# Attention scores of a two-layer decoder trunk from three or four products a head instead of four, with the weight splits held back earlier

## The chip, the core and the metric

The kernel runs on one core of one Trainium2 chip. The metric is the device time of one execution in microseconds (us); lower is better. Before the change the median of three runs was 938.75 us, the lowest 937.65 and the highest 941.82.

## What is computed

A trunk of two layers for one sequence of 256 tokens of width 1024, in float32. Cut to its order:

```python
for layer in range(2):
    h = h + 0.5 * swiglu(rms_norm(h, ffn1_norm[layer]), ...)     # width 2816
    hn = rms_norm(h, mix_norm[layer])
    h = h + (ab_mixer(hn, ...) if layer == 0 else c_mixer(hn, ...))
    h = h + 0.5 * swiglu(rms_norm(h, ffn2_norm[layer]), ...)
return rms_norm(h, final_norm)
```

The first mixer has 8 causal attention heads of width 64 (three dilated windows, folded into one additive mask of log counts) beside a gated branch (gelu, norm, causal mixing of positions). The second mixer has 16 causal heads of width 64. In both, a head needs scores q k^T, a masked softmax, and the weighted sum of v. With 256 queries in two blocks of 128, block 0 attends to 128 keys and block 1 to 256.

## The kernel before, in words

**Numbers in two parts.** TensorE multiplies in its fast float32 form (fp32r), which drops bits. So each operand is held as a rounded high part and a low part (the rest), and `mm3` (L265 to L268) adds three products, high with high, low with high, high with low. ScalarE (ACT) makes the high part by a copy, VectorE (DVE) the low part by a subtraction.

**The weight stream.** `Stream` (L115) loads the weights in chunks of 1 MB in the order in which they are used, into three raw buffers, by DMA from the SP queue. `split_parts` (L147) turns a chunk into its two parts (`whi` by ACT on L172, `wlo` by DVE on L173), in one of four buffers each. A chunk can be split when the chunk four places ahead of it has been used (`pump`, L186). `hold` (L196) stops splitting; `release` (L200) splits one chunk, or lets all that is due go again, and places these instructions behind some given ones.

**The order of the work.** A mixer is written as a sequence of projections on TensorE (PE), with attention steps put between them by hand: `Slots` (L747) counts steps, each of some 2.7 us of projection matmuls (half that in the last four), and at each step calls what was put down for it: `scores` of a head, `turn` of a head (three transposes of its probabilities and their split into `pth` and `ptl`), `weighted` of a pair of heads (their products with v, split into `mixh` and `mixl`). The tile framework then orders each engine's instructions; every engine works its list in order. In the first mixer, steps 0 to 3 are `first_tiles`, 4 to 11 two `token_block`s, 12 to 19 four weight chunks of two steps each, and 20 to 27 `project` (L388), the output projection. In the second, steps 4 to 7 and 16 to 19 are token blocks, 24 to 31 `project`. `project` ends with `nxt.pair` (L308), which adds the result to the residual (L312, DVE) and makes the next stage's `xTh` (L302, ACT) and `xTl` (L305, DVE); the next feed-forward stage starts on these.

**The scores.** A pair of heads shares a tile of 128 partitions, 64 for each head. `put_q` (L665) makes the head's `q` tile: the high part on its own 64 partitions (L672, ACT) and a copy of it on the other 64 (L674, GpSimd, called POOL); and a tile `ql` with the low part on its own 64 partitions and zeros on the others (L673, DVE). `put_k` (L677) makes `k`: the high part on the head's own partitions (L683, ACT), the low part on the others (L685, POOL or DVE). So one product with `q` gives high by high plus high by low, and one with `ql` gives low by high. `scores` (L690) does both for each of two query blocks, four matmuls with 256 columns (L700, L701). Then for each block DVE adds the mask and takes the row's minimum of the negated scores (L704), ACT takes the exponential and its sum (L707), DVE the reciprocal (L710), and POOL, or DVE for the last heads, scales the probabilities (L714).

**Before the change** the first mixer puts scores of heads 0 to 3 at steps 6 to 9 and of 4 to 7 at 20, 20, 21, 21, turns at 10, 10, 12, 12, 22, 22, 23, 23, `hold` at 19, and releases at 21 (one chunk, behind the scores of head 7), 22 (one, behind turn 5) and 25 (all, behind the last `weighted`). The second mixer has no hold of its own.

Of the kernel before, what the change touches and what calls it, by code (L numbers as in the profile page):

```python
# [35 lines left out]
LINE, SHIFT = 64, 16  # L36
# [188 lines left out]
def trunk(ctx: ExitStack, tc: tile.TileContext, a, out):  # L225
    nc = tc.nc
# [418 lines left out]
    def make_attention(mp, mask_cols, nheads, v, mix, rows=False):  # L645

        qs, ks, probs, pts = {}, {}, {}, {}
        pairs, flying = (4, 5) if rows else (2, 4)
        seconds = [mp.tile([128, 2 * S + LINE], F32R, name=f"ql{i}") for i in range(pairs)]
        for t in seconds:  # L650
            for j in range(2):
                o = slice(64 - j * 64, 128 - j * 64)
                nc.gpsimd.memset(t[o, SHIFT + j * S : SHIFT + (j + 1) * S].bitcast(F32), 0.0)  # L653
        mask = mp.tile([128, 384], F32, name="mask")
        nc.scalar.dma_start(mask, a["consts"][:, mask_cols])

        def scaled(bk):
            t = mp.tile([128, S], F32, name="qk", bufs=3)
            nc.vector.tensor_mul(t, bk[:, :S], norm["row"])
            return t  # L660

        def sides(j):
            return slice(j * 64, j * 64 + 64), slice(64 - j * 64, 128 - j * 64)

        def put_q(p, bk):  # L665

            t = bk[:, :S] if rows else scaled(bk)
            qq = mp.tile([128, 2 * S + LINE], F32R, name="q", bufs=pairs)
            for j in range(2):
                q, ql = (u[:, SHIFT + j * S : SHIFT + (j + 1) * S] for u in (qq, seconds[p % pairs]))  # L670
                r, o = sides(j)
                nc.scalar.activation(q[r, :], t[r, :], AF.Copy)  # L672
                nc.vector.tensor_sub(ql[r, :], t[r, :], q[r, :].bitcast(F32))  # L673
                nc.gpsimd.tensor_copy(q[o, :], q[r, :].bitcast(F32))  # L674
                qs[2 * p + j] = (q, ql)

        def put_k(p, bk):  # L677

            t = scaled(bk)
            for j in range(2):  # L680
                k = mp.tile([128, S], F32R, name=f"k{j}", bufs=pairs)
                r, o = sides(j)
                nc.scalar.activation(k[r, :], t[r, :], AF.Copy)  # L683
                engine = nc.vector if p > 1 and not rows else nc.gpsimd
                engine.tensor_sub(k[o, :], t[r, :], k[r, :].bitcast(F32))  # L685
                ks[2 * p + j] = k
            if p == 1 or p == 3 and not rows:

                nc.scalar.activation(wk.tile([128, 2], F32, name="l")[:, :1], t[:, :1], AF.Exp, scale=0.0)

        def scores(h):
            q, ql = qs.pop(h)
            k = ks.pop(h)
            sc = bank()
            pr = mp.tile([128, 384], F32, name="pr", bufs=flying)
            nm = wk.tile([128, 2], F32, name="nm")
            l = wk.tile([128, 2], F32, name="l")
            for b in range(2):
                bs = slice(b * 128, b * 128 + 128)
                nc.tensor.matmul(sc[:, b * S : (b + 1) * S], q[:, bs], k, start=True, stop=False)  # L700
                nc.tensor.matmul(sc[:, b * S : (b + 1) * S], ql[:, bs], k, start=False, stop=True)  # L701
            for b, (c0, n) in enumerate(((0, 128), (128, 256))):
                cs = slice(c0, c0 + n)
                nc.vector.tensor_tensor_reduce(pr[:, cs], sc[:, b * S : b * S + n], mask[:, cs],  # L704
                                               norm["score"][:, b : b + 1] if rows else -SCALE, 3e38,
                                               op0=ALU.add, op1=ALU.min, accum_out=nm[:, b : b + 1])
                power = nc.scalar.activation(pr[:, cs], pr[:, cs], AF.Exp, bias=nm[:, b : b + 1], scale=-1.0,  # L707
                                             accum_out=l[:, b : b + 1])
            rl = wk.tile([128, 2], F32, name="rl")
            nc.vector.reciprocal(rl, l)  # L710
            for b, (c0, n) in enumerate(((0, 128), (128, 256))):
                cs = slice(c0, c0 + n)
                engine = nc.gpsimd if h < nheads - (4 if rows else 2) else nc.vector
                share = engine.tensor_scalar(pr[:, cs], pr[:, cs], rl[:, b : b + 1], None, op0=ALU.mult)  # L714
            probs[h] = pr
            return power, share

        def turn(h):
            p, j = divmod(h, 2)
            pr = probs.pop(h)  # L720
            tp = bank()
            for i in range(3):
                nc.tensor.transpose(tp[:, i * 128 : (i + 1) * 128], pr[:, i * 128 : (i + 1) * 128], ident)  # L723
# [100 lines left out]
    def ab_mixer(phase):  # L824
        with tc.tile_pool(name="mp", bufs=1) as mp:
# [4 lines left out]
            put_q, put_k, scores, turn, weighted = make_attention(mp, slice(0, 384), 8, v, mix)  # L830
# [38 lines left out]

            slots = Slots()  # L870
            slots.at((15, 16, 16, 17), mixing)
            slots.at((19,), lambda _: st.hold())
            slots.at((6, 7, 8, 9, 20, 20, 21), scores)
            slots.at((21,), lambda _: st.release(tc, scores(7), True))
            slots.at((10, 10, 12, 12, 22), turn)
# [19 lines left out]
    def c_mixer(phase):  # L895
        with tc.tile_pool(name="mp", bufs=1) as mp:
# [93 lines left out]
```

## Time and profile before

| | |
|---|---|
| median of the runs | 938.75 us |
| profiled execution, whole | 937.01 us |
| its span, first to last instruction | 935.3 us |
| PE busy | 927.7 us (99%) |
| DVE busy | 612.1 us (65%) |
| ACT busy | 499.2 us (53%) |
| POOL busy | 83.0 us (9%) |
| first matmul after the first mixer starts at | 277.24 us of the span |
| first matmul after the second mixer starts at | 748.22 us of the span |

The span is the time between the first and the last instruction of one profiled execution; 1.71 us of the whole lie around it. A row of the timeline has the start in us from the span's start, the time in us, engine, line, operation, output and inputs, and the count of instructions that it merges. A matmul's row shows its own time from start to modelled end, which overlaps with the next; what one matmul costs on a busy PE is the distance to the next one's start.

### The profile page before, as it was taken

How to read it: one execution, taken by the hardware profiler on the slowest of the kernel's cores; microseconds unless marked ns; L12 is line 12 of the kernel's file. 1: busy time of each engine (PE TensorE's matmuls, PEld its weight loads, DVE VectorE, ACT ScalarE, POOL GpSimd, SP SyncE). 2: the span in 40 equal slices, each digit the busy share in tenths (PEclk: the TensorE clock that was granted, in tenths of full speed). 3: DMA queues.
4: the chain of work that ended last, by engine and by line, in shares of the span. 5: the costliest groups of instructions: out<-in, count | busy, mean ns of one | idle time of the engine just before them, and what ended most of it. 6: DMA issues, size and time to landing. Idle time of an engine off the chain costs nothing.

```text
span 935.3 us, 18101 instructions
## 1 busy us (share of the span) xinstructions
PE 927.7 (99%) x7655; PEld 907.4 (97%) x7655; DVE 612.1 (65%) x892; ACT 499.2 (53%) x782; POOL 83.0 (9%) x114
## 2 busy tenths in 40 slices
PE   9999999999999999999999999999999999999997
PEld 9999999999999999999999999999999999999886
DVE  7866556676888666555756665567787786656543
ACT  7744444468667454444454544456786665445431
POOL 0000000034210000000000000002574000000000
PEclk9999999999999999999999999999999999999999
DMA  8755554665336555555555555556543377555521
GB/s 320 281 212 181 189 194 162 223 222 180 136 136 226 188 211 188 183 175 206 204 184 200 204 180 170 203 184 220 177 139 136 137 243 269 186 188 210 190 90 46
DMA packets 28305, 176.99 MB, mean 189 GB/s; under 512 B 3264, under 2 KB 4672, under 8 KB 9152
## 3 DMA queue, kind: packets, MB, share of 16 engines
q1 hardware_dynamic: 26928, 173.65, 52.5%
q10 hardware_dynamic: 1296, 2.18, 0.7%
q8 instruction: 60, 0.98, 0.4%
q14 instruction: 21, 0.17, 0.0%
HBM read 173.72 MB, written 2.10 MB: 188 GB/s over the span
## 4 chain that ended last, share of the span: by engine, by line
PE 98%; issue 1%; DMA 0%; ACT 0%; SPq 0%; DVE 0%; POOLq 0%; POOL 0%
PE bank L266 30%; PE bank L267 30%; PE bank L268 30%; PE bank L567 2%; PE bank L571 2%; PE bank L568 2%; PE bank L723 1%; PE bank L700 1%; PE bank L701 1%; DMA x<-in_x 0%; PE bank L343 0%; PE bank L859 0%; PE bank L361 0%; PE bank L455 0%; PE bank L456 0%
## 5 line engine op out<-in xcount | busy, mean ns | idle before, releaser
L172 ACT ACTIVATE whi<-raw 128x1024 fp32r<-128x1024 f32 (+3 forms) x352 | 330.5, 985 | 350.1 <-issue 282.9
L173 DVE TENSOR_TENSOR wlo<-raw,whi 128x1024 fp32r<-128x1024 f32 (+3 forms) x352 | 389.6, 1141 | 126.7 <-ACT whi L172 125.8
L266 PE MATMUL bank<-xTh,whi 128*128 128x256 f32 x1616 | 447.9, 277 | 0.0
L267 PE MATMUL bank<-xTl,whi 128*128 128x256 f32 x1616 | 446.7, 276 | 0.0
L268 PE MATMUL bank<-xTh,wlo 128*128 128x256 f32 x1616 | 446.6, 276 | 0.0
L267 PEld LDWEIGHTS bank<-xTl,whi 128*128 128x128 f32 x1616 | 303.5, 188 | 0.2
L266 PEld LDWEIGHTS bank<-xTh,whi 128*128 128x128 f32 x1616 | 303.5, 188 | 0.0
L268 PEld LDWEIGHTS bank<-xTh,wlo 128*128 128x128 f32 x1616 | 303.5, 188 | 0.0
L267 PE MATMUL bank<-hTl,whi 128*128 128x256 f32 x528 | 145.8, 276 | 0.0
L266 PE MATMUL bank<-hTh,whi 128*128 128x256 f32 x528 | 145.8, 276 | 0.0
L268 PE MATMUL bank<-hTh,wlo 128*128 128x256 f32 x528 | 145.8, 276 | 0.0
L266 PEld LDWEIGHTS bank<-hTh,whi 128*128 128x128 f32 x528 | 99.1, 188 | 0.0
L268 PEld LDWEIGHTS bank<-hTh,wlo 128*128 128x128 f32 x528 | 99.1, 188 | 0.0
L267 PEld LDWEIGHTS bank<-hTl,whi 128*128 128x128 f32 x528 | 99.1, 188 | 0.0
L506 DVE TENSOR_TENSOR hm<-gs,bank 128x512 f32<-128x512 f32 x44 | 30.1, 687 | 77.7 <-PE bank L268 77.3
L503 DVE TENSOR_TENSOR gs<-bank,row 128x512 f32<-128x512 f32 x44 | 30.0, 689 | 47.8 <-PE bank L268 47.8
L266 PE MATMUL bank<-mixh,whi 128*128 128x256 f32 x128 | 35.3, 281 | 0.0
L267 PE MATMUL bank<-mixl,whi 128*128 128x256 f32 x128 | 35.1, 277 | 0.0
L268 PE MATMUL bank<-mixh,wlo 128*128 128x256 f32 x128 | 35.0, 277 | 0.0
L714 POOL TENSOR_SCALAR pr<-pr,rl 128x128 f32<-128x128 f32 (+1 forms) x36 | 30.8, 870 | 25.2 <-DVE rl L710 14.1
L653 POOL MEMSET ql<- 64x256 f32 x12 | 3.7, 307 | 328.7 <-ACT whi L172 170.3
L567 PE MATMUL bank<-whi,hTh 128*128 128x512 f32 x80 | 31.1, 389 | 0.0
(134 smaller groups left out, 877.4 us busy)
## 6 DMA issues: line engine op xcount, KB each, us to landing
raw<-in_weights SPq DMA_DIRECT2D x149, 1024.0 KB, 4.9
raw<-in_weights SPq DMA_DIRECT2D x12, 768.0 KB, 4.4
raw<-in_weights SPq DMA_DIRECT2D x6, 512.0 KB, 6.5
x<-in_x SPq DMA_DIRECT2D x4, 264.0 KB, 4.0
raw<-in_weights SPq DMA_DIRECT2D x4, 256.0 KB, 4.3
away<-xn SPq DMA_DIRECT2D x2, 512.0 KB, 5.5
xr<-away SPq DMA_DIRECT2D x8, 128.0 KB, 5.7
fg<-in_final_norm ACTq DMA_DIRECT2D x1, 512.0 KB, 3.7
```

The costliest lines, as they stand in the source:

```text
L172: nc.scalar.activation(hi, r, AF.Copy)
L173: nc.vector.tensor_sub(lo, r, hi.bitcast(F32))
L266: nc.tensor.matmul(p, sh, mh, start=start, stop=False)
L267: nc.tensor.matmul(p, sh, ml, start=False, stop=False)
L268: nc.tensor.matmul(p, sl, mh, start=False, stop=stop)
L503: nc.vector.tensor_mul(g, both(pg), twice(norm["row"]))
L506: nc.vector.tensor_mul(hm, g, both(pu))
L567: nc.tensor.matmul(banks[t, h], sh, w[0][kw][:, cs], start=k == 0, stop=False)
L568: nc.tensor.matmul(banks[t, h], sh, w[1][kw][:, cs], start=False, stop=False)
L571: nc.tensor.matmul(banks[t, h], sl, w[0][kw][:, cs], start=False, stop=k == FT - 1)
L700: nc.tensor.matmul(sc[:, b * S : (b + 1) * S], q[:, bs], k, start=True, stop=False)
L714: share = engine.tensor_scalar(pr[:, cs], pr[:, cs], rl[:, b : b + 1], None, op0=ALU.mult)
```

## The change

Three edits.

1. **Scores.** In the first mixer for heads 0 to 3, in the second for all 16, `q` holds the high part on the head's own 64 partitions and the low part on the other 64 (one DVE subtraction, no POOL copy, no `ql`). `k` has two halves: in the first the high part on both 64s (ACT, then a POOL copy), in the second the low part on the head's own partitions (a POOL subtraction) and zeros on the others (memset once). One product of `q` with the first half gives high by high plus low by high; one with the second half gives high by low. Query block 0 needs 128 keys only, so one matmul takes the first 128 columns of both halves side by side (256 columns), and a new DVE add (`added`) joins its second 128 columns with the mask before the reduction. Block 1 takes two matmuls. Heads 2 and 10 of the second mixer keep four matmuls and no `added`. Heads 4 to 7 of the first mixer are as before.
2. **First mixer.** `hold` at step 17 instead of 19; the releases stay.
3. **Second mixer.** Scores of heads 7 to 11 one step later; turns of heads 4 and 5 at step 15 instead of 16, of 8 and 9 at 21 instead of 20, of 10 and 11 at 23 instead of 22; `weighted` of pair 2 at 17 instead of 18, of pair 4 at 23 instead of 22, of pair 5 at 25 instead of 24. `hold` at step 24, one chunk released behind the scores of head 15 (step 25), the rest behind turn 15 (step 27).

```diff
         pairs, flying = (4, 5) if rows else (2, 4)
-        seconds = [mp.tile([128, 2 * S + LINE], F32R, name=f"ql{i}") for i in range(pairs)]
-        for t in seconds:
-            for j in range(2):
-                o = slice(64 - j * 64, 128 - j * 64)
+        keys = [[mp.tile([128, 2, S], F32R, name=f"k{i}{j}") for j in range(2)] for i in range(pairs)]
+        seconds = [] if rows else [mp.tile([128, 2 * S + LINE], F32R, name=f"ql{i}") for i in range(2)]
+        for j in range(2):
+            o = slice(64 - j * 64, 128 - j * 64)
+            for pair in keys:
+                nc.gpsimd.memset(pair[j][o, 1].bitcast(F32), 0.0)
+            for t in seconds:
                 nc.gpsimd.memset(t[o, SHIFT + j * S : SHIFT + (j + 1) * S].bitcast(F32), 0.0)
...
+        def early(p):
+
+            return rows or p < 2
...
                 nc.scalar.activation(q[r, :], t[r, :], AF.Copy)
-                nc.vector.tensor_sub(ql[r, :], t[r, :], q[r, :].bitcast(F32))
-                nc.gpsimd.tensor_copy(q[o, :], q[r, :].bitcast(F32))
-                qs[2 * p + j] = (q, ql)
+                if early(p):
+                    nc.vector.tensor_sub(q[o, :], t[r, :], q[r, :].bitcast(F32))
+                    qs[2 * p + j] = q, None
+                else:
+                    ql = seconds[p - 2][:, cs]
+                    nc.vector.tensor_sub(ql[r, :], t[r, :], q[r, :].bitcast(F32))
+                    nc.gpsimd.tensor_copy(q[o, :], q[r, :].bitcast(F32))
+                    qs[2 * p + j] = q, ql
...
-                k = mp.tile([128, S], F32R, name=f"k{j}", bufs=pairs)
+                k = keys[p % pairs][j]
                 r, o = sides(j)
-                nc.scalar.activation(k[r, :], t[r, :], AF.Copy)
-                engine = nc.vector if p > 1 and not rows else nc.gpsimd
-                engine.tensor_sub(k[o, :], t[r, :], k[r, :].bitcast(F32))
+                nc.scalar.activation(k[r, 0], t[r, :], AF.Copy)
+                if early(p):
+                    nc.gpsimd.tensor_copy(k[o, 0], k[r, 0].bitcast(F32))
+                    nc.gpsimd.tensor_sub(k[r, 1], t[r, :], k[r, 0].bitcast(F32))
+                else:
+                    nc.vector.tensor_sub(k[o, 0], t[r, :], k[r, 0].bitcast(F32))
                 ks[2 * p + j] = k
...
             q, ql = qs.pop(h)
+            if rows and h in (2, 10):
+
+                ql = q
...
-            for b in range(2):
-                bs = slice(b * 128, b * 128 + 128)
-                nc.tensor.matmul(sc[:, b * S : (b + 1) * S], q[:, bs], k, start=True, stop=False)
-                nc.tensor.matmul(sc[:, b * S : (b + 1) * S], ql[:, bs], k, start=False, stop=True)
+            if ql is None:
+                nc.tensor.matmul(sc[:, :S], q[:, :128], k[:, :, :128], start=True, stop=True)
+                nc.tensor.matmul(sc[:, S : 2 * S], q[:, 128:], k[:, 0], start=True, stop=False)
+                nc.tensor.matmul(sc[:, S : 2 * S], q[:, 128:], k[:, 1], start=False, stop=True)
+                added = mp.tile([128, 128], F32, name="added", bufs=2)
+                nc.vector.tensor_add(added, sc[:, 128:S], mask[:, :128])
+            elif ql is q:
+                added = mask[:, :128]
+                for i in range(2):
+                    for b in range(2):
+                        nc.tensor.matmul(sc[:, b * S : (b + 1) * S], q[:, b * 128 : (b + 1) * 128], k[:, i],
+                                         start=i == b == 0, stop=i == b == 1)
+            else:
...
-                nc.vector.tensor_tensor_reduce(pr[:, cs], sc[:, b * S : b * S + n], mask[:, cs],
+                nc.vector.tensor_tensor_reduce(pr[:, cs], sc[:, b * S : b * S + n], mask[:, cs] if b else added,
...
-            slots.at((19,), lambda _: st.hold())
+            slots.at((17,), lambda _: st.hold())
...
-            slots.at((5, 6, 7, 8, 12, 13, 14, 15, 16, 17, 18, 19, 24, 24, 25, 25), scores)
-            slots.at((9, 9, 11, 11, 16, 16, 18, 18, 20, 20, 22, 22, 26, 26, 27, 27), turn)
-            slots.at((11, 13, 18, 20, 22, 24, 28, 29), weighted)
+            slots.at((5, 6, 7, 8, 12, 13, 14, 16, 17, 18, 19, 20, 24, 24, 25), scores)
+            slots.at((24,), lambda _: st.hold())
+            slots.at((25,), lambda _: st.release(tc, scores(15), True))
+            slots.at((9, 9, 11, 11, 15, 15, 18, 18, 21, 21, 23, 23, 26, 26, 27), turn)
+            slots.at((27,), lambda _: st.release(tc, turn(15)))
+            slots.at((11, 13, 17, 20, 23, 25, 28, 29), weighted)
```

More of the change, by code (lines that the diff above doesn't have):

```diff
@@ L669, in put_q @@
             for j in range(2):
-                q, ql = (u[:, SHIFT + j * S : SHIFT + (j + 1) * S] for u in (qq, seconds[p % pairs]))
+                cs = slice(SHIFT + j * S, SHIFT + (j + 1) * S)
+                q = qq[:, cs]
                 r, o = sides(j)
                 nc.scalar.activation(q[r, :], t[r, :], AF.Copy)
-                nc.vector.tensor_sub(ql[r, :], t[r, :], q[r, :].bitcast(F32))
-                nc.gpsimd.tensor_copy(q[o, :], q[r, :].bitcast(F32))
-                qs[2 * p + j] = (q, ql)
+                if early(p):
[6 more added lines that the diff above has]
+                    qs[2 * p + j] = q, ql
         def put_k(p, bk):
@@ L697, in scores @@
             l = wk.tile([128, 2], F32, name="l")
-            for b in range(2):
-                bs = slice(b * 128, b * 128 + 128)
-                nc.tensor.matmul(sc[:, b * S : (b + 1) * S], q[:, bs], k, start=True, stop=False)
-                nc.tensor.matmul(sc[:, b * S : (b + 1) * S], ql[:, bs], k, start=False, stop=True)
+            if ql is None:
[11 more added lines that the diff above has]
+            else:
+                added = mask[:, :128]
+                for b in range(2):
+                    bs = slice(b * 128, b * 128 + 128)
+                    nc.tensor.matmul(sc[:, b * S : (b + 1) * S], q[:, bs], k[:, 0], start=True, stop=False)
+                    nc.tensor.matmul(sc[:, b * S : (b + 1) * S], ql[:, bs], k[:, 0], start=False, stop=True)
             for b, (c0, n) in enumerate(((0, 128), (128, 256))):
                 cs = slice(c0, c0 + n)
-                nc.vector.tensor_tensor_reduce(pr[:, cs], sc[:, b * S : b * S + n], mask[:, cs],
+                nc.vector.tensor_tensor_reduce(pr[:, cs], sc[:, b * S : b * S + n], mask[:, cs] if b else added,
                                                norm["score"][:, b : b + 1] if rows else -SCALE, 3e38,
```

## Prediction, made before the changed kernel was run

> **What bounds the kernel.** First the page: busy shares, granted clock, the chain that ended last. Then the windows of the two mixers, the only stages that the change touches.
>
> ```profile
> span 935.3 us, 18101 instructions
> PE 927.7 (99%) x7655; PEld 907.4 (97%) x7655; DVE 612.1 (65%) x892; ACT 499.2 (53%) x782; POOL 83.0 (9%) x114
> PEclk9999999999999999999999999999999999999999
> PE 98%; issue 1%; DMA 0%; ACT 0%; SPq 0%; DVE 0%; POOLq 0%; POOL 0%
> 195.00:290.00 95.00, 94.88 (x722) 90.09 (x722) 75.41 (x162) 66.84 (x146) 26.53 (x33) 1.00 0.45 158
> 645.00:765.00 120.00, 120.00 (x932) 114.86 (x931) 95.83 (x224) 86.09 (x189) 47.03 (x57) 1.00 0.47 165
> ```
>
> TensorE is the bound, at full clock, in both mixers too (94.88 of 95 us and 120 of 120). So an edit is worth what it takes from PE's row of matmuls, less what PE newly waits for. DVE is 79% to 80% busy in these windows (75.41 of 95, 95.83 of 120): work added there can come late. A busy PE can hide a wait shorter than a matmul's own 0.28 us, so I read waits from distances between starts.
>
> **The matmuls that go.** Before, a head has four; after, 4 heads of the first mixer and 14 of the second have three: 18 fewer.
>
> ```profile
> 655.72 0.28 PE L700 MATMUL bank<-k,q 128*128 128x256 f32 x1
> 656.19 0.40 PE L266 MATMUL bank<-whi,xTh 128*128 128x512 f32 x1
> ...
> 679.11 0.28 PE L700 MATMUL bank<-k,q 128*128 128x256 f32 x1
> 679.56 0.28 PE L266 MATMUL bank<-xTh,whi 128*128 128x256 f32 x1
> ...
> L266 PE MATMUL bank<-pth,vth 128*128 128x256 f32 x12 | 3.4, 280 | 0.0
> ```
>
> Four take 0.47 us in a token block (656.19 - 655.72) and 0.45 us elsewhere, 0.118 and 0.113 each. Eight of the 18 lie in token blocks, or after one: 8 x 0.118 + 10 x 0.113 = **-2.07 us**. One of the three reads two strips of 128 columns; the `pth` row above is such a matmul and takes 280 ns like the others, so I add nothing for it. In token blocks the matmuls after a head run a little slow; a new count can move that either way, and I allow 0.5 us on both sides for it. The POOL copy moves from `q` to `k`, 24 before and 24 after (16 of the second mixer and 4 + 4 of the first), and memsets lie where POOL idles (it is 9% busy). The new DVE add counts below, where something waits for it.
>
> **Hold at step 17, what it frees.** Chunk C, the third of the output projection, is no longer split before the scores of heads 4 to 7.
>
> ```profile
> 249.97 1.22 DVE L173 TENSOR_TENSOR wlo<-raw,whi 128x1024 fp32r<-128x1024 f32 x1
> 251.10 0.41 DVE L659 TENSOR_TENSOR qk<-bank,row 128x256 f32<-128x256 f32 x1
> 252.00 0.87 DVE L685 TENSOR_TENSOR k<-qk,k 64x256 fp32r<-64x256 f32 x2 [0.48 <-ACT k L683]
> ...
> 252.17 0.28 PE L268 MATMUL bank<-mixh,wlo 128*128 128x256 f32 x1
> 252.57 0.36 PE L700 MATMUL bank<-k,q 128*128 128x256 f32 x1
> 252.76 0.28 PE L701 MATMUL bank<-k,ql 128*128 128x256 f32 x1
> 252.88 0.28 PE L700 MATMUL bank<-k,q 128*128 128x256 f32 x1
> ```
>
> PE starts head 4 at 252.57, 0.40 after the matmul before it, and then takes 0.19 for one more: 0.36 us over two steps of 0.113. It waits for `k`, which DVE makes at 252.00 behind that half of the split (1.22). Without it `k` comes a microsecond sooner and the wait goes: **-0.36**.
>
> **Hold at step 17, what it defers.** The releases stay, so each lets out the chunk before the one it did: C, D, and at the last two at once, E and F. In the built order of the changed kernel DVE has four `wlo` halves there instead of two, all ahead of the residual adds.
>
> ```profile
> 271.38 2.36 DVE L173 TENSOR_TENSOR wlo<-raw,whi 128x1024 fp32r<-128x1024 f32 x2 [0.66 <-ACT whi L172]
> 273.77 1.29 DVE L312 TENSOR_TENSOR x<-bank,x 128x512 f32<-128x512 f32 x2
> ...
> 277.90 0.87 DVE L305 SCALAR_TENSOR_TENSOR xTl<-x,gT,xTh 128x256 fp32r<-128x256 f32 x2
> ...
> 279.05 0.28 PE L267 MATMUL bank<-xTl,whi 128*128 128x256 f32 x1
> ```
>
> The residual add starts as the second half ends (271.38 + 2.36 = 273.74, add at 273.77), and DVE has no idle time from there to the `xTl` of k = 4 and 5, done at 278.77. PE wants k = 5 at 279.05: 0.28 us to spare. Two more halves cost 2.36 us, so the adds start at 276.1 and that `xTl` is done at 281.1. PE waits 2.36 - 0.28 = **+2.1 us** in the first matmuls of the feed-forward stage. ACT is no later than DVE (its halves take 1.0). C and D come in time: C takes the place where D's `wlo` was, done before its first use. Bounds: 1.0 (one half slips behind the adds) to 2.4.
>
> **Turns of heads 4 and 5 a step sooner, behind longer score chains.**
>
> ```profile
> 687.66 0.17 DVE L710 RECIPROCAL rl<-l 128x2 f32<-128x2 f32 x1
> 688.02 1.50 POOL L714 TENSOR_SCALAR pr<-pr,rl 128x128 f32<-128x128 f32 x2
> 689.69 0.28 PE L700 MATMUL bank<-k,q 128*128 128x256 f32 x1
> 693.37 0.82 PE L723 MATMUL bank<-ident,pr 128*128 128x128 f32 x6
> ...
> L864 DVE TENSOR_TENSOR tmp<-bank,sbias 128x128 f32<-128x128 f32 x8 | 1.9, 280 | 0.3 <-POOL mixl L868 0.3
> L673 DVE TENSOR_TENSOR ql<-bank,q 64x256 fp32r<-64x256 f32 x16 | 6.7, 421 | 0.8 <-ACT q L672 0.4
> ```
>
> Before, head 5's probabilities are scaled at 688.02 to 689.52 and turned at 693.4, 3.9 us later. Now the turn stands at step 15, where head 7's scores stood (689.69), 0.34 sooner for three matmuls gone: 689.35, head 5's from 689.7. And its chain is longer: `added` for heads 4 and 5 (the L864 row is the like: 0.28 each), and head 4's second reduction now behind the second subtraction for `q` (0.42). That is at most 0.98; I take 0.85, since part fits into idle time. Reciprocal at 688.5, scaling done at 690.25; PE has three transposes to do meanwhile and waits **+0.55** (0 to 1.2). A rule weighed here: the Trainium skill, "SBUF — State Buffer", section "Who interferes with whom", says that a DVE instruction with two SBUF inputs and a GpSimd one that reads SBUF exclude each other for the whole instruction. By it a `wlo` in the way would add its 1.2 to 1.5 us; the built order puts none behind that reciprocal, so by the rule the sum is the same, and if it is wrong on that, 1.5 us more.
>
> **Second mixer, last steps.** Turns 14 and 15 stand at step 27 in both. Splits no longer stand between the scores of heads 14 and 15, so their probabilities are ready; now chunk F's split stands behind the turns' `pth` and `ptl`, not before.
>
> ```profile
> 730.81 0.82 PE L723 MATMUL bank<-ident,pr 128*128 128x128 f32 x6
> 734.21 0.90 PE L723 MATMUL bank<-ident,pr 128*128 128x128 f32 x6
> 734.29 2.01 ACT L172 ACTIVATE whi<-raw 128x1024 fp32r<-128x1024 f32 x2 [0.52 <-PE bank L267]
> 735.38 2.36 DVE L173 TENSOR_TENSOR wlo<-raw,whi 128x1024 fp32r<-128x1024 f32 x2 [0.76 <-ACT whi L172]
> 738.59 0.41 DVE L271 TENSOR_TENSOR mixl<-bank,mixh 64x256 fp32r<-64x256 f32 x1
> 739.45 0.43 DVE L271 TENSOR_TENSOR mixl<-bank,mixh 64x256 fp32r<-64x256 f32 x1 [0.45 <-ACT mixh L271]
> 739.81 0.28 PE L266 MATMUL bank<-mixh,whi 128*128 128x256 f32 x1
> 739.93 0.38 PE L267 MATMUL bank<-mixl,whi 128*128 128x256 f32 x1
> 740.15 0.29 PE L268 MATMUL bank<-mixh,wlo 128*128 128x256 f32 x1
> ```
>
> Six transposes take 0.90 at 734.21 and 0.82 at 730.81: the wait of 0.08 goes, **-0.08**. After the turns F's `wlo` begins some 1.3 us later than before (behind two `pth` and two `ptl`), so the last `mixl` of pair 6 comes 0.1 to 0.7 us later against PE. Before, PE already waits for it once: 739.93 to 740.15 is 0.22, 0.11 over. So **+0.3** (0 to 0.7).
>
> **Sum.** -2.07 - 0.36 + 2.1 + 0.55 - 0.08 + 0.3 = +0.44 us. The profiled execution, 937.01 us (span 935.3 and 1.71 around it), becomes 937.45; it lies 1.74 below the median of the runs, 938.75, from which I forecast **939.2 us**: no change, for a measurement of this kernel can tell about 0.5% (4.7 us) from none.
>
> **The rivals.**
>
> *The new waits don't come; only matmuls go.* For it: PE has waited almost nowhere in 920 us, and the terms +2.1 and +0.55 rest on slack that I read to 0.3 us. Against it: the order of the four `wlo` ahead of the adds is fixed, and the adds followed the split by 0.03 us. All that then stays is -2.07 - 0.36 - 0.08 and the 0.11 wait: -2.6, **936.1 us**.
>
> *Slower: POOL comes late for the turn of heads 6 and 7 (step 18).* Head 7's scores move to step 16, its turn stays; behind head 5's scaling POOL has four passes for `k`, head 6's scaling, four more for `k`, and head 7's scaling.
>
> ```profile
> L674 POOL CAST q<-q x24: 392/480/1897, 201.6 to 715.9; 64x256 fp32r<-64x256 f32 x24
> L685 POOL TENSOR_TENSOR k<-qk,k x20: 727/739/1754, 202.9 to 722.8; 64x256 fp32r<-64x256 f32 x20
> L714 POOL TENSOR_SCALAR pr<-pr,rl x36: 602/919/1937, 211.5 to 709.6; 128x128 f32<-128x128 f32 x18, 128x256 f32<-128x256 f32 x18
> ```
>
> At medians that is 4 x 0.480 + 4 x 0.739 + 4 x 0.919 = 8.6 us, from 690.25 to 698.8. PE wants head 7 near 701.2: after 690.6 come three steps of 24 matmuls' time (2.7 each), three heads of 0.35, one `weighted` of 1.0 and head 6's transposes, 0.33. At the longest of each row it is 22.4 us: 11 us late. It decides from 10.9 us. At 15 us PE waits 4.1 more, and the time is **943.3 us**. The rule of the Trainium skill above is what would make these passes long; 1.897 against 0.392 agrees with it, for a `wlo` pass takes 1.2 us. Against it: long passes are rare, or the medians would not lie at the shortest.
>
> *The stacked product doesn't save.* If the matmul on two strips took as long as two, 18 x 0.115 come back: +2.5 in all, **941.3 us**. The `pth` row speaks against it.
>
> **Chances.** Forecast within 1.5 us 0.60; waits don't come 0.22; POOL late 0.11; no saving 0.07. Range for 8 in 10: from the first rival with the 0.5 of the token blocks, 935.6, up to between the third and the second, 942.2. Over 0.5% faster is beyond every case (-2.6 is 0.28%) but for the scatter of the runs: 0.03. Over 0.5% slower needs POOL's rival past its price, or terms at their upper ends with a scatter like that of the slowest run: 0.07. Within: 0.90.
>
> **What the profile after would show.** 7637 matmuls, three to a head. The wait at 252 gone. Four `wlo` in a row before the first L312 of the first mixer, and PE waiting for `xTl` near 278, 2 us in pieces. A wait of about half a microsecond inside the transposes of head 5, none before heads 6 and 7. A pair 6 `mixl` that PE waits for by 0.3. I am wrong if `xTl` is there in time, if L714 of head 7 ends after 701, or if matmuls outside the mixers change their pace.

## The result, and the profile after

The changed kernel takes 940.66 us (median of 20 runs; 940.33 to 941.25) where the kernel before, in 20 runs beside them, takes 937.58. The ratio is 1.003, with a 95% interval of 1.0023 to 1.0037: slower by 0.30%, some 2.8 us. That is inside the 0.5% called no change and inside the forecast's range, but the forecast had +0.4. The forecast of 939.2 us lies only 1.5 us from the measured time, and part of that is luck: it was built on a median of 938.75 us, where the runs beside this one have 937.58. As a change, +0.4 was far too small; several terms of the sum are wrong, and the experiments below are about those. Of several kernels here, the kernel before included, single executions took some 3 to 13 us longer than the rest, and a ratio counts them in, so where ratio and median differ the median is closer to what the traces show.

Page of the changed kernel: span, busy time, chain.

```profile
span 939.2 us, 18072 instructions
PE 927.7 (99%) x7637; PEld 906.1 (96%) x7637; DVE 617.6 (66%) x910; ACT 498.6 (53%) x782; POOL 82.3 (9%) x118
PE 89%; DVE 4%; ACT 3%; issue 1%; POOL 1%; DMA 0%; SPq 0%; POOLq 0%; ACTq 0%; DVEq 0%
```

Its waits of PE from 240 to 770 us (in total, times, longest). The same view of the kernel before lists none there.

```profile
PE bank L756 <- POOL pr L747: 2.0, 3, 0.9
PE bank L756 <- DVE mixl L271: 1.7, 1, 1.7
```

Eighteen matmuls have gone (7637), yet the chain of PE has fallen from 98% to 89%: PE now waits, and others have become part of what ends last. The span grew by 3.9 us. I split that by the distances between starts of matmuls, at the same points of both programs.

**First mixer.** Before head 4 the wait is gone: PE runs straight from the projection into the scores.

```profile
252.17 0.28 PE L268 MATMUL bank<-mixh,wlo 128*128 128x256 f32 x1
252.28 0.28 PE L733 MATMUL bank<-k,q 128*128 128x256 f32 x1
```

Behind the mixer the four halves stand in one row, the adds follow, and PE waits at the first `xTl`. DVE, then PE:

```profile
271.01 4.63 DVE L173 TENSOR_TENSOR wlo<-raw,whi 128x1024 fp32r<-128x1024 f32 x4 [0.66 <-ACT whi L172]
275.67 1.29 DVE L312 TENSOR_TENSOR x<-bank,x 128x512 f32<-128x512 f32 x2
276.94 0.89 DVE L305 SCALAR_TENSOR_TENSOR xTl<-x,gT,xTh 128x256 fp32r<-128x256 f32 x2
```
```profile
276.96 0.38 PE L266 MATMUL bank<-xTh,whi 128*128 128x256 f32 x1
277.48 0.39 PE L267 MATMUL bank<-xTl,whi 128*128 128x256 f32 x1
...
278.23 0.44 PE L266 MATMUL bank<-xTh,whi 128*128 128x256 f32 x2
...
288.96 0.50 PE L343 MATMUL bank<-ones,acc 128*128 128x1 f32 x4
```
```profile
288.12 0.50 PE L343 MATMUL bank<-ones,acc 128*128 128x1 f32 x4
```

The last fence is of the kernel before. From the first feed-forward matmul to the sums (L343) it took 288.12 - 277.24 = 10.88 us for 96 matmuls; now 288.96 - 276.96 = 12.00. With 0.1 on the matmul ahead, and 0.1 at the spread transposes later, this place costs 1.3, not 2.1. The two L266 in a row at 278.23 tell why: the framework put products of the second tile, with the first four k, between those of the first, so that PE has work while `xTl` of the higher k is made. Of the 1.3, waits are 0.8; 0.3 is that the next 67 matmuls run at 0.118 us and not 0.113 ((288.96 - 281.06) / 67).

```profile
281.06 0.28 PE L266 MATMUL bank<-xTh,whi 128*128 128x256 f32 x1
```

**Second mixer, turns of heads 5, 7 and 15** (PE; then one row of DVE in the kernel before; then DVE and POOL in the changed kernel):

```profile
690.97 0.33 PE L756 MATMUL bank<-ident,pr 128*128 128x128 f32 x1 [0.53 <-POOL pr L747]
691.87 0.33 PE L756 MATMUL bank<-ident,pr 128*128 128x128 f32 x1 [0.57 <-POOL pr L747]
704.01 0.44 PE L756 MATMUL bank<-ident,pr 128*128 128x128 f32 x2 [0.90 <-POOL pr L747]
738.46 0.52 PE L756 MATMUL bank<-ident,pr 128*128 128x128 f32 x3 [1.74 <-DVE mixl L271]
```
```profile
685.23 1.94 DVE L173 TENSOR_TENSOR wlo<-raw,whi 128x384 fp32r<-128x384 f32 x2
```
```profile
688.58 1.49 DVE L173 TENSOR_TENSOR wlo<-raw,whi 128x1280 fp32r<-128x1280 f32 x1
689.99 0.16 DVE L743 RECIPROCAL rl<-l 128x2 f32<-128x2 f32 x1
...
700.89 2.35 DVE L173 TENSOR_TENSOR wlo<-raw,whi 128x1024 fp32r<-128x1024 f32 x2
...
735.50 2.36 DVE L173 TENSOR_TENSOR wlo<-raw,whi 128x1024 fp32r<-128x1024 f32 x2 [0.20 <-ACT whi L172]
737.89 0.43 DVE L271 TENSOR_TENSOR mixl<-bank,mixh 64x256 fp32r<-64x256 f32 x1
```
```profile
700.99 2.96 POOL L747 TENSOR_SCALAR pr<-pr,rl 128x256 f32<-128x256 f32 x1
```

Each of the three has a `wlo` in front of it, in another way. Head 5: the reciprocal stands behind a half of 1.49 us on DVE. That half alone is not what is new: before the change it stood ahead of that reciprocal too (685.23, with a smaller piece, 1.94 us for both). All of DVE's chain there comes later. Head 7: POOL's second scaling pass takes 2.96 us, beside two halves on DVE (700.89 to 703.24), where the median pass of that line is 0.92. Head 15: its transposes write the PSUM bank that held the output of pair 5, and the last reader of that bank, the second `mixl`, stands on DVE behind two halves. In starts the three cost 1.54, 1.12 and 1.9 us.

The sum: -2.09 (matmuls), -0.36, +1.3, +1.54, +1.12, +1.9, +0.1 (pair 6) = +3.5; another 0.47 lies ahead of 28 us, where the x load landed later in that one execution.

### The profile page after: what moved, and what is told of

The parts are those of the page before. It is cut to its first block, busy times and chain, and to the rows that moved or that the text cites. A ratio compares the mean times of both kernels' runs of the same rounds, so it can differ in the third digit from the quotient of the medians.

```text
span 939.2 us, 18072 instructions
## 1 busy us (share of the span) xinstructions
PE 927.7 (99%) x7637; PEld 906.1 (96%) x7637; DVE 617.6 (66%) x910; ACT 498.6 (53%) x782; POOL 82.3 (9%) x118
## 4 chain that ended last, share of the span: by engine, by line
PE 89%; DVE 4%; ACT 3%; issue 1%; POOL 1%; DMA 0%; SPq 0%; POOLq 0%; ACTq 0%; DVEq 0%
PE bank L267 27%; PE bank L266 27%; PE bank L268 27%; DVE wlo L173 2%; PE bank L571 2%; PE bank L568 2%; PE bank L567 2%; ACT whi L172 2%; ACT pr L740 1%; POOL pr L747 1%; DVE pr L737 0%; DMA x<-in_x 0%; DVE q L682 0%; PE bank L756 0%; ACT k L696 0%
## 5 line engine op out<-in xcount | busy, mean ns | idle before, releaser
L266 PE MATMUL bank<-xTh,whi 128*128 128x256 f32 x1616 | 447.8, 277 | 0.0
L266 PEld LDWEIGHTS bank<-xTh,whi 128*128 128x128 f32 x1616 | 303.4, 188 | 0.2
L266 PE MATMUL bank<-hTh,whi 128*128 128x256 f32 x528 | 145.7, 276 | 0.0
L266 PEld LDWEIGHTS bank<-hTh,whi 128*128 128x128 f32 x528 | 99.1, 188 | 0.0
L266 PE MATMUL bank<-mixh,whi 128*128 128x256 f32 x128 | 35.1, 281 | 0.0
L747 POOL TENSOR_SCALAR pr<-pr,rl 128x128 f32<-128x128 f32 (+1 forms) x36 | 31.1, 877 | 29.2 <-DVE rl L743 28.9
L654 POOL MEMSET k<- 64x256 f32 x12 | 3.2, 306 | 328.0 <-ACT whi L172 169.9
L271 DVE TENSOR_TENSOR hTl<-hm,hTh 128x512 fp32r<-128x512 f32 x44 | 30.1, 685 | 2.1 <-ACT hTh L271 2.1
```

What stands on the lines that cost most here:

```text
L266: nc.tensor.matmul(p, sh, mh, start=start, stop=False)
L271: return nc.scalar.activation(hi, src, AF.Copy), nc.vector.tensor_sub(lo, src, hi.bitcast(F32))
```

## The experiments

Each run stands against the kernel before on the same chip; a ratio has its 95% interval. "Slots" are the steps of the second mixer.

**1. The scores alone, the slots alone, the hold alone.** Theory: scores -2, slots and hold what is lost. Rival: the scores themselves cost it.

```diff
 (scores_only: the changed kernel with)
-            slots.at((17,), lambda _: st.hold())
+            slots.at((19,), lambda _: st.hold())
...
+            slots.at((5, 6, 7, 8, 12, 13, 14, 15, 16, 17, 18, 19, 24, 24, 25, 25), scores)
+            slots.at((9, 9, 11, 11, 16, 16, 18, 18, 20, 20, 22, 22, 26, 26, 27, 27), turn)
+            slots.at((11, 13, 18, 20, 22, 24, 28, 29), weighted)
```

> The changed scores with every slot and the hold where they stood before the change. Theory: the 18 matmuls save 2.07 us and the longer chain from scores to turn is hidden by the old slots (3.9 us for head 5), so the run is 1.7 to 2.1 us faster than the kernel before (ratio 0.998), 7637 matmuls, and PE waits for no scaled probabilities at heads 4 to 7; all that the changed kernel loses comes from its slots and holds. Rival (the new scores themselves cost it: more DVE and POOL work ahead of other things, or a two-strip matmul that takes longer): no gain over the kernel before, or up to 2 us slower.

Measured: 938.40 us, ratio 1.001 (0.9998 to 1.0022). No gain. Waits of PE, then what stands on DVE ahead of turn 14:

```profile
PE bank L756 <- DVE pr L747: 1.1, 2, 0.8
PE bank L756 <- POOL pr L747: 0.5, 1, 0.5
...
```
```profile
729.58 0.49 DVE L722 TENSOR_TENSOR added<-bank,mask 128x128 f32<-128x128 f32 x2
729.98 2.35 DVE L173 TENSOR_TENSOR wlo<-raw,whi 128x1024 fp32r<-128x1024 f32 x2
732.25 0.34 DVE L737 CUSTOM_DVE_ANT_0 pr<-bank,added,score 128x128 f32<-128x128 f32 x1
```

In starts PE loses 1.6 at turns 14 and 15, 0.8 at turn 7, 0.2 at head 7's scores and 0.6 at head 4 of the first mixer: 3.2, against 0.5 before. The rival holds: the new scores eat their own saving, without any new slot. The DVE rows show a way that I had not thought of. The two adds are done, but the framework then puts two halves of a split between them and the reductions that need them; before, the reductions of head 14 stood ahead of the halves.

```diff
 (slots_only: the kernel before with the changed second mixer's slots, hold and releases; hold at 19 in the first)
```

> The kernel before with the second mixer's slots, hold and releases of the changed kernel, its own four products and the first mixer's hold at 19. Theory (the wait at turn 15 is for the bank, whose reader stands behind the released halves, whatever the scores): 1.9 us at turn 15 as in the changed kernel, 0.6 at turn 5 (the chain without the add and the moved q is 0.85 shorter), none at turn 7: +2.4 us, ratio 1.0026. Rival (the slots cost only behind the longer chains): within 0.5 of the kernel before. Rival (the slots hurt as much at heads 5 and 7): +4.

Measured: 937.71 us, ratio 1.0007 (0.9992 to 1.0023), span 935.6. Its only wait:

```profile
PE bank L700 <- DVE k L685: 0.2, 1, 0.2
```

That is head 4's, as before the change. No wait at turns 5, 7 or 15. My theory falls: the slots cost nothing by themselves, the bank of turn 15 included. The halves ahead of pair 5's second `mixl` are there too, but DVE starts them at 731.44 and not at 735.50. Turn 15 starts at 734.87, before that `mixl` ends (735.06), so it does not wait for that bank there; which bank it writes the trace does not say.

```diff
 (hold17_only: the kernel before with)
-            slots.at((19,), lambda _: st.hold())
+            slots.at((17,), lambda _: st.hold())
```

> The kernel before with the hold of the first mixer at step 17 and nothing else. Theory from the profile after: -0.36 (the wait for head 4's k goes) and +1.2 to +1.4 at the first feed-forward matmuls (0.8 in pieces, since the built order puts products of the second tile between those of the first, 0.3 for matmuls that then run at 0.118 instead of 0.113, 0.1 at the spread transposes): +0.9 us, ratio 1.001. Rival (the term as predicted, 2.1 us of waiting): +1.7 us. Rival (nothing comes of it alone): 0.

Measured: 938.84 us, ratio 1.0036 (1.0011 to 1.0061), span 936.3 against 935.3. The interval is too wide to tell 0.9 from 1.7, but the trace does:

```profile
277.08 0.38 PE L266 MATMUL bank<-xTh,whi 128*128 128x256 f32 x1
277.60 0.39 PE L267 MATMUL bank<-xTl,whi 128*128 128x256 f32 x1
```

The first `xTl` is 0.4 late (0.52 between starts), as in the changed kernel, and the built order has the second tile's products between too. The span grows by 1.0: the mechanism belongs to the hold alone, at the lesser size. One part differs: the 96 matmuls to the sums take 11.70 us here and 12.00 in the changed kernel, for most of the 67 run at 0.113 again.

**2. Without the add.** If DVE's add is the cause, the waits at turns 5 and 15 go with it. Two ways: leave it out (the output then lacks one product), or let PE add.

```diff
 (no_added: scores_only with)
-                added = mp.tile([128, 128], F32, name="added", bufs=2)
-                nc.vector.tensor_add(added, sc[:, 128:S], mask[:, :128])
+                added = mask[:, :128]
```

> The changed scores in the old slots with the old hold, as in the run of the scores alone, but without the DVE add: the first 128 keys of query block 0 are reduced with the mask only, so the high-by-low product is left out of that block. Theory: in the built order the add puts the reductions of heads 14 and 15 behind two wlo halves; without it they stand ahead again, and the 1.5 us at turns 14 and 15 go, while the 0.7 at turn 7 and the 0.4 at head 7's scores, both waits for POOL, stay: 1.5 us faster than the run of the scores alone, -0.7 against the kernel before. Rival (the waits come from the k passes on POOL): nothing changes, +0.8. Rival (PE is ahead of DVE by the matmuls saved, and waits that much at whatever comes next): the 1.5 move to another place.

Measured: 937.18 us, ratio 0.9992 (0.9984 to 1.0001), span 935.1 against 936.5 with the add.

```profile
PE bank L755 <- POOL pr L746: 1.1, 1, 1.1
PE bank L755 <- DVE pr L746: 0.6, 1, 0.6
```

The add was worth 1.4 us of span. As expected POOL's wait at turn 7 stays, larger (1.3 in starts); the 1.6 at turns 14 and 15 fell to 0.9 and did not go; head 7's scores and, not expected, head 4 of the first mixer wait no more. What is left is the rival that PE is ahead. POOL ends head 7's scaling at 700.34 (before the change 700.15), and DVE starts the reduction of head 12 at 723.84 (before 723.92) and keeps the order of the kernel before from there to turn 15; but PE comes to turn 6 at 698.74 and not at 700.48, and to turn 14 at 733.23 and not at 734.21. So even without the add PE waits 2.2 us, where the kernel before waits 0.5, and hardly any of the 2.07 that the matmuls save is left.

```diff
 (narrow_new: the changed kernel, hold at 19, with)
-                nc.tensor.matmul(sc[:, :S], q[:, :128], k[:, :, :128], start=True, stop=True)
+                nc.tensor.matmul(sc[:, :128], q[:, :128], k[:, 0, :128], start=True, stop=False)
+                nc.tensor.matmul(sc[:, :128], q[:, :128], k[:, 1, :128], start=False, stop=True)
...
+                added = mask[:, :128]
```

> The changed kernel without the add and complete: query block 0 takes two products of 128 columns, one with each half of k, that accumulate in place; so four matmuls a head, two of them half as wide. Second mixer's slots as in the changed kernel, hold at 19 in the first mixer. Theory (the add and what it does to DVE's order make the waits at turns 5 and 15): the built order of DVE is then, step by step, nearly that of the run of the slots alone, and those two waits go; at turn 7 POOL's k passes remain, 0 to 1.1 us. The price of a product of 128 columns is not in the profile: at 0.113 (like 256 columns) the matmuls save nothing and the time is that of the kernel before, 0 to +1; at half, 2.0 us are saved and it is 1 to 2 us faster than the kernel before. Rival (the moved k passes on POOL and not the add are behind the waits): turn 5 and turn 15 still wait 1.5 and 1.9, +3.

Measured: 937.56 us, ratio 0.9999 (0.999 to 1.0008). Waits, and one head's products:

```profile
PE bank L756 <- POOL pr L747: 0.5, 1, 0.5
```
```profile
678.55 0.22 PE L718 MATMUL bank<-k,q 128*128 128x128 f32 x1
678.60 0.28 PE L719 MATMUL bank<-k,q 128*128 128x128 f32 x1
678.72 0.33 PE L720 MATMUL bank<-k,q 128*128 128x256 f32 x1
678.89 0.28 PE L721 MATMUL bank<-k,q 128*128 128x256 f32 x1
```

The waits at turns 5 and 15 are gone, with the changed slots and the changed work for `q` and `k` on POOL and DVE still there; turn 7 keeps 0.7. But this run takes two things away, the add and PE's saved time (below). For turn 5 the starts tell them apart: PE comes to turn 4 at 689.94 in the changed kernel, at 690.01 in slots_only and at 689.16 here, and the reciprocal of head 5 at 689.99, 687.99 and 687.55. Against slots_only PE is hardly earlier, and DVE is 2.0 later. So at turn 5 it is DVE's longer chain, with the add and the order around it. For turn 15 these runs leave open how much is that and how much PE's lead. The products give nothing back: by the medians of 18 heads the four take 0.058 + 0.113 + 0.169 + 0.120 = 0.46 us, as four of 256 columns did (0.45 to 0.47). The first of the two narrow ones is followed at half the distance, and the ones behind it come later by as much.

**3. One wait at a time.** Is a wait that is removed a gain?

```diff
 (release_behind_pair5: the changed kernel with)
-            slots.at((25,), lambda _: st.release(tc, scores(15), True))
...
+            slots.at((25,), lambda _: st.release(tc, weighted(5), True))
...
 (dve_scales_5_7: the changed kernel with)
-                engine = nc.gpsimd if h < nheads - (4 if rows else 2) else nc.vector
+                engine = nc.gpsimd if h < nheads - (4 if rows else 2) and not (rows and h in (5, 7)) else nc.vector
```

> The changed kernel, with the chunk that was released behind the scores of head 15 released behind the weighted sum of pair 5 in the same step, so that the last mixl of pair 5 stands ahead of the two wlo halves. Theory: turn 15 waits because the bank that it writes is still to be read by that mixl, which stands behind the halves (1.9 us); the wait goes, and the run is 1.5 to 1.9 us faster than the changed kernel, +1.3 against the kernel before. Rival (turn 15 waits for the probabilities of head 15): no change, +3.1. Rival (the chunk itself comes late for its first product at step 28 in place of it): PE waits there for whi or wlo by 0.5 to 1.

> The changed kernel, with the probabilities of heads 5 and 7 of the second mixer scaled by DVE and not by POOL. Theory: POOL's two passes (1.5 us and more) and, at head 7, its queue are the last links; DVE does them in 0.55, so the wait at turn 5 falls from 1.5 to about 0.6 and the one at turn 7 goes: 2.0 us faster than the changed kernel, +1.1 against the kernel before. Rival (DVE's queue is the late part, the reciprocal behind a wlo of 1.5 us): turn 5 keeps over 1 us, and turn 7 gets a wait on DVE of its own: no change, +3.

Measured: 941.02 us, ratio 1.0053 (1.0035 to 1.0072), and 940.75 us, ratio 1.0039 (1.0026 to 1.0052). Waits of the first, then of the second:

```profile
PE bank L756 <- POOL pr L747: 2.0, 3, 0.9
PE bank L266 <- DVE ptl L271: 0.7, 1, 0.7
PE bank L266 <- ACT mixh L271: 0.4, 1, 0.4
```
```profile
PE bank L756 <- DVE mixl L271: 1.8, 1, 1.8
PE bank L718 <- POOL k L699: 1.3, 1, 1.3
...
```

Both mechanisms are confirmed and neither pays. With `mixl` ahead of the halves turn 15 waits no more: in the changed kernel it was the bank. But PE then waits 1.1 for `ptl` and 0.9 for `mixh` and what follows, in starts: 2.0 in place of the 1.9. With DVE scaling, turn 5 falls from 1.54 to 0.77 and turn 7 goes; then PE, 2 us earlier, waits 1.5 for the `k` of head 13, which it had not met before.

```diff
 (act_copies: the changed kernel, second mixer only, with)
-                    nc.gpsimd.tensor_copy(k[o, 0], k[r, 0].bitcast(F32))
+                    nc.scalar.activation(k[o, 0], t[r, :], AF.Copy)
 (old_heads_4_7: the changed kernel with scores of 7 at step 15, turns 4 and 5 at 16, weighted 2 at 18)
```

> The changed kernel, with the copy of k's high part onto the other 64 partitions made by ACT straight from qk in the second mixer, and not by POOL. Theory: head 7's scaled probabilities are late because POOL works off four passes for the k of pair 4 first; POOL then has half of them, and the 1.1 us wait at turn 7 goes, while the 1.5 us at turn 5 stays, for there POOL idles until DVE's reciprocal: 1.1 us faster than the changed kernel, +2.0 against the kernel before. Rival (DVE is what is late at both, with POOL only behind it): both waits stay. Rival (ACT's 16 more copies push its exponentials): a new wait of up to 1 us elsewhere.

> The changed kernel, with head 7's scores at step 15, the turns of heads 4 and 5 at 16 and the weighted sum of pair 2 at 18 as before the change. Theory: the waits for scaled probabilities at head 5 (1.5 us) and head 7 (1.1 us) come from these slots; both go, 2.6 us faster than the changed kernel, about +0.5 us against the kernel before. Rival (the wait at head 7 comes from the longer chain and a slow POOL, whatever the slots): only the first goes, +1.6 us against the kernel before. Rival (waits shift to a later place): +3.

Measured: 944.32 us, ratio 1.0094 (1.0063 to 1.0125), and 945.16 us, ratio 1.0078 (1.0054 to 1.0101). Both are misses. Waits with ACT's copies:

```profile
PE bank L721 <- DVE ptl L271: 2.0, 1, 2.0
PE bank L759 <- POOL pr L750: 1.8, 3, 0.9
...
```

With ACT's 16 copies turn 7's wait halves (0.5), turn 5's grows to 2.2, and a new one of 2.2 comes at step 24. In the other run turn 5 no longer waits, but turn 7 stands where POOL, after the four passes for `k`, scales beside two halves: the rival on POOL from the prediction, 2.6 and 0.8 us (rows in the last section). Not all of its 945.16 us is that. The six times lie between 942.55 and 949.48, the profiled one is 947.26, and in it the last stage, from the sums at 765.41 to the last matmul at 939.01, takes 173.6 us, 4.0 more than the same matmuls of the changed kernel (763.04 to 932.62), with no wait listed. And both runs show TensorE's clock fall after a wait. The window from 704 to 707 us of the old places (time, PE, PEld, DVE, ACT, POOL, clock, DMA):

```profile
704.00:707.00 3.00, 3.00 (x10) 2.61 (x11) 1.12 (x4) 1.00 (x3) 1.27 (x2) 0.50 0.83 325
```

**4. Versions meant to beat both.**

```diff
 (extra_release: the changed kernel, first mixer, with)
+            slots.at((20,), lambda _: st.release(tc, scores(5), True))
...
 (combined1: scores_only with act_copies, hold at 17 with that release, and)
-            if rows and h in (2, 10):
+            if rows and h in (2, 10, 12, 13, 14, 15):
 (best3: scores_only, head 7 scaled on DVE, and)
-            if rows and h in (2, 10):
+            if rows and h in (2, 7, 10, 12, 13, 14, 15):
```

> The changed kernel, with one more release in the first mixer, of one chunk behind the scores of head 5 at step 20, so that each later release lets out the chunk that it did before the change. Theory: the four wlo halves ahead of the residual adds become two, PE no longer waits for xTl, and the 0.36 at head 4 stays won: 1.3 us faster than the changed kernel, +1.8 against the kernel before. Rival (two halves now stand between the scores of heads 5 and 6, so turns 6 and 7 come late): PE waits there by 0.5 to 1 instead.

> The three-product scores for heads 0 to 3 of the first mixer and for the second mixer's heads but 2, 10 and 12 to 15 (four products, no added), the second mixer's slots of before without a hold, the copy of k by ACT in the second mixer, hold at 17 in the first mixer with the extra release. Theory (matmuls save what is predicted where DVE and POOL are given as little new work as before): 14 matmuls fewer, 1.6 us, and 0.36 at head 4, no new wait: 1.9 us faster than the kernel before, ratio 0.998. Rival (the longer chain from score to turn costs as much wherever it stands): no faster than the kernel before.

> The scores alone in the old slots with the old hold, with four products and no added for heads 7 and 12 to 15 too, and head 7's scaling on DVE. In the built order the last steps of the second mixer are those of the kernel before. Theory: 13 matmuls fewer save 1.5 us; the wait at head 4 grows by 0.28, head 7's scores wait up to 0.4, turns 7, 14 and 15 wait no more than before: 0.8 us faster than the kernel before, ratio 0.999. Rival (PE ahead of DVE by what it saves waits that much at the next place, whatever it is): no faster, 0 to +1.

Measured: 940.46 us, ratio 1.0029 (1.0018 to 1.004); 943.04 us, 1.007 (1.005 to 1.009); 938.36 us, 1.0006 (0.9997 to 1.0014). The extra release takes the wait for `xTl` away and puts one for `ptl` and for what follows it, 1.2 us in starts, into the weighted sums of pairs 2 and 3. In combined1 PE waits 1.2 for POOL's `k` and 1.8 for the probabilities of head 15. In best3, whose built order of the last steps is that of the kernel before:

```profile
PE bank L756 <- DVE pr L747: 1.5, 1, 1.5
...
```

Turn 15 waits all the same, now for the probabilities. By step 24 PE is 0.7 us earlier than before (scores of head 12 at 721.76, before 722.49), and DVE 1.1 later (their reduction at 725.03, before 723.92). Together that is the wait. None of the twelve runs is clearly faster than the kernel before.

## Why the prediction was right, and where it was not

- **Matmuls, -2.07.** Right: 4 and 14 fewer, -0.49 and -1.6. The stacked product takes no longer than another; that rival is out.
- **Hold frees the k of head 4, -0.36.** Right; in hold17_only PE goes straight on into head 4 too. But narrow_new and no_added show another way to it: without the add, with the hold at 19, head 4 does not wait either.
- **Hold defers, +2.1.** The mechanism was right: four halves in a row, then the adds, then PE waiting for `xTl`. The size was off: 1.3. The adds came 1.9 later, not 2.36, and above all PE's order was taken over from the kernel before, while the framework had mixed the second tile into the first. The built order of PE shows it.
- **Turns 4 and 5 earlier, +0.55.** Measured 1.54. The step that failed is the size of the delay on DVE: 0.85 us, from 687.66 to 688.5; it was 2.33, to 689.99, while PE came to turn 4 at 689.94 and not at 689.35. Of the 2.33, 1.24 was there before head 4's reductions began: the `mixl` ahead of them starts at 682.09, before at 680.85 (0.58 of that PE has too, with the scores of head 4 at 679.69, before 679.11). Another 0.89 came between that and head 4's reciprocal, about the size foreseen, and 0.20 behind it. The prediction looked for halves behind head 5's reciprocal, found none, rightly, and did not ask whether those ahead of it would run as early as before. In slots_only, with the same slots, the reciprocal starts at 687.99 and nothing waits. So the slots alone were not the cause, as I had argued: they cost it only together with the new scores.
- **Second mixer, last steps, -0.08 and +0.3.** The failing step is that only the probabilities and pair 6's `mixl` were followed. The wait of 1.9 is for a PSUM bank; its reader stands behind the released halves. Pair 6's `mixl` was late by 0.1 more.
- **The rival on POOL at turn 7** (0.11) came, at 1.12 and not 4.1. POOL's own row there was one pass of 2.96 beside two halves. The Trainium skill, "SBUF — State Buffer", "Who interferes with whom", by which the two exclude each other for the whole instruction, agrees with this row (0.92 + 2.04, and the halves take 2.35), and with the same scaling in old_heads_4_7. The prediction named the rule for this rival, but its price came from the longest rows, and the two halves were not looked for beside this pass.
- **The sum** had +0.44 and the trace has +3.5: turns 5, 7 and 15 cost 4.1 more than it gave them, the deferred halves and pair 6 1.0 less. By two of its own signs the prediction was wrong: the scaling of head 7 (now L747) ended at 703.95, after 701, and matmuls behind the first mixer changed their pace. The measured time still lies near the forecast because the runs' base was lower and because neither sum is large.

What the experiments say about the cause: the three-product scores are a trade. PE saves 0.113 us a head; DVE gets an add in the chain from scores to turn. At the places where PE takes the probabilities, the other engines' chains end hardly before PE needs them, as the waits that move show, so PE saves time only to wait for it. The wait goes to whatever is next: removed at turns 5 and 7 it is met at head 13, removed at turn 15 at `ptl` and `mixh`. Two parts are shown. PE's lead alone comes back as waiting, since the others' rows stay where they were (no_added). The add costs 1.4 us of span on top in the old slots (scores_only against no_added), and in the new ones DVE's later chain makes the wait at turn 5. Whether the add's 0.28 us or the other order that the framework builds around it weighs more stays open; no run had the add with the old order. So does the share of each part at turn 15.

## What to carry to other kernels

When PE is 99% busy and another engine 80% in the same stage, count an instruction taken from PE as a gain only if the other engines' chains can come earlier by as much, and get no longer by it; here three products and an add of 0.28 us a head saved 2.1 us of matmuls and brought 2.7 us of new waits (scores_only). Where a framework orders the engines, read its built order again, for every engine, PE too: with a small new operation, large ones can stand at other places, as the two halves ahead of head 14's reductions do. And ask of a moved transpose not only where its input comes from, but who has last to read the bank that it will write.

## What the runs showed of the hardware

**The clock falls after little waiting.** Rows of PE in old_heads_4_7, then of PE and of a window in act_copies:

```profile
702.94 0.33 PE L756 MATMUL bank<-ident,pr 128*128 128x128 f32 x1 [2.48 <-POOL pr L747]
703.84 0.69 PE L756 MATMUL bank<-ident,pr 128*128 128x128 f32 x2 [0.57 <-POOL pr L747]
...
704.75 0.63 PE L267 MATMUL bank<-ptl,vth 128*128 128x512 f32 x1
705.18 0.63 PE L268 MATMUL bank<-pth,vtl 128*128 128x512 f32 x1
```
```profile
691.57 0.33 PE L759 MATMUL bank<-ident,pr 128*128 128x128 f32 x1 [0.92 <-POOL pr L750]
692.47 0.44 PE L759 MATMUL bank<-ident,pr 128*128 128x128 f32 x2 [0.57 <-POOL pr L750]
```
```profile
693.40:696.40 3.00, 3.00 (x9) 2.28 (x8) 1.79 (x9) 2.39 (x7) 2.16 (x3) 0.51 0.49 147
```

In the first, after waits of 2.48 and 0.57 us, 512-column products start every 0.43 us (705.18 - 704.75) and not 0.23, at a granted clock of 0.50 for 3 us. In the second, waits of 0.92 and 0.57 are followed by 0.51 for 3 us. In the changed kernel a single 1.74, and 0.53 with 0.57, were not. The Trainium skill, "TensorE: Matmul & The Clock Gate", Part 1, speaks of an idle window of about 3.4 us before the clock is halved; the 0.43 us agrees with its cold figure for 512 columns (426.7 ns), but no idle stretch here was that long, so the measurement decides: waits that add up to 1.5 us in 3 can be enough. Waiting alone does not decide it, though. From 735.9 to 739.3 us of the changed kernel PE is busy for 1.66 of 3.40 us, with 16 matmuls, and the clock stays at 1.00; from 690.0 to 693.4 of act_copies it is busy for 1.82 of 3.40, with 10, and the clock falls. What does decide it these runs leave open.

**A product of 128 columns** starts the next after 0.058 us, yet two of them in a group of four saved nothing.

**The same matmuls have two paces.** In the changed kernel, behind the wait for `xTl`, 67 in a row ran at 0.118 us in place of 0.113, until the sums. Behind the same wait in hold17_only most ran at 0.113. In the kernel before, 54 in a row ran at 0.118 from 462.66 us to the sums, and in the profiled execution of old_heads_4_7 903 in a row, from 772.75 to 879.11 us; no wait is listed in the 20 us ahead of either, and the granted clock from 773 to 879 us is 1.00. Those 903 are the 4.0 us of its last stage. What sets the pace stays open.
